# A product in the Mamba-2 chunks on VectorE instead of GpSimd, with new orders of issue at the head and in the last output projection

## The chip, the cores and the metric

One core of a Trainium2 chip runs the whole kernel. The metric is the device time of one execution in microseconds (us); of several executions the median counts. TensorE is called PE in the profile, VectorE DVE, ScalarE ACT, GpSimd POOL and SyncE SP.

## The reference

One decoder layer (DEPTH is 1) on 1024 tokens of width 1024, everything in float32. `h @ w_in` gives the columns for two branches: a convolution branch (a gated product, a causal depthwise convolution of 31 taps, a layer norm, silu, a projection) and a Mamba-2 branch (chunks of 128 tokens, 32 heads in 4 groups). Both are gated, added and projected, then a layer norm; a convolutional gated MLP and another layer norm follow.

```python
def conformer_branch(u_glu, dw_w, dw_b, ln_g, ln_b, w_out):
    a, g = jnp.split(u_glu, 2, axis=-1)
    v = a * jax.nn.sigmoid(g)
    v = causal_dwconv(v, dw_w, dw_b)
    v = jax.nn.silu(layer_norm(v, ln_g, ln_b))
    return v @ w_out

def ssd_chunked(x, dt, a_head, bm, cm):
    ...
    y_diag = jnp.einsum("bcgrls,bcsgrp->bclgrp", cb[:, :, :, None] * decay, xs)
    ...
    y_off = jnp.einsum("bclgn,bcgrpn,bcgrl->bclgrp", cc, prev, jnp.exp(a_cs))
    return (y_diag + y_off).reshape(b, t, h, p)

def reference(x, ...):
    h = layer_norm(x, ln_in_g, ln_in_b)
    for l in range(DEPTH):
        u = h @ w_in[l]
        u_glu, z, xbc, dt_raw, gate_a, gate_b = split_in(u)
        y_a = conformer_branch(u_glu, ...)
        y_b = ssd_branch(z, xbc, dt_raw, ...)
        mix = (jax.nn.sigmoid(gate_a) * y_a + jax.nn.sigmoid(gate_b) * y_b) @ w_o[l]
        h = layer_norm(DN_ALPHA * h + mix, ln1_g[l], ln1_b[l])
        ffn = conv_ffn(h, w_ffn_up[l], ffn_dw_w[l], ffn_dw_b[l], w_ffn_down[l])
        h = layer_norm(DN_ALPHA * h + ffn, ln2_g[l], ln2_b[l])
    return h
```

The line of `y_off` is the one that the change is about: C times the carried decays `exp(a_cs)`, which then meets the state that a chunk inherits.

## The kernel before

Every large matrix product is done in three passes: each float32 operand is split into a high part (fp32r, a rounded copy) and a low part (the remainder), and high x high, high x low and low x high are added up in one PSUM bank. These are lines 190, 191 and 192 (`mm3`), 128x512 each. A block of weights of 128x1024 is made by `weights` (line 151 on): SyncE loads it, ScalarE casts it (line 156), and VectorE, or whichever engine is given, subtracts (line 161).

The tokens go in two halves of 512 (`hh` 0 and 1). In each half the input projection, the 31-tap convolution (line 558, one VectorE operation per tap and 128 channels), and the mixer run together. The mixer works on 4 groups of 4 chunks each, 32 chunks in all. In a chunk of a group ScalarE makes `ab`'s exponentials for 8 heads; `m` (line 622, then line 642 on VectorE, multiplied by `cbm`, the masked product of C and B) feeds the matmuls of line 647, and `ce` (line 625 on ScalarE, then line 626, multiplied by C) those of line 650, which read the state. Every chunk but the first of the sequence has a `ce`: 28 of them. Line 632 makes `xs`, 637 `xsd`, 657 to 662 the new state, 665 and 675 the output with the skip and the gate z.

After the mixer each half has its "combine": the convolution's layer norm over channels. GpSimd adds up the channels (lines 795, 797), PE spreads the mean by a matmul (line 802), VectorE subtracts it (804), ScalarE squares (809), GpSimd adds (810), PE spreads the variance (814), and root, reciprocal, scaling, silu and the split into `sT` follow (815 to 820, 206, 207). Then the blocks `w_co` of the convolution branch's projection read `sT`. PE fills the time in between with the gate columns (`w_gb`) and the Mamba-2 branch's projection (`w_sp`).

At the head, `ln_in_first` normalises the first 512 tokens, in tiles t0 to t3 of 128, and transposes them: pair 0 is t0 and t1, pair 1 t2 and t3. Per tile: statistics (line 231, two of them), aggregation (250), root on ScalarE (251), reciprocal (254), the normalised tile `xh` (306 on VectorE or 326 on ScalarE), eight transposes on PE (328), the high part `hT_h` (341 or 347), the whole value `f` and the low part `hT_l` (353, two operations for a pair). `first_columns` multiplies the first three column blocks (line 492, 128x256): 48 matmuls with `hT_h` of pair 0, 24 with `hT_l`, then the same for pair 1. The lists kept on the way name operations: `in_order` begins with the root of t0, the root of t1, `hi` (the last `hT_h` by VectorE), `lo` and `lo_2` (the two of line 353), and the roots of t2 and t3; `parts_of[4:8]` are the statistics of t2 and t3; `los[2]` is the subtraction of the third column block, w_c_16, the only one of the three that VectorE makes; GpSimd makes the other two.

The last output projection, `out_proj_pairs`, works on the second half's tiles in two pairs (r4, r5 and r6, r7 in the text; the trace calls them all r). Each pair has four PSUM banks, 4 x 2 weight blocks `w_wo`, the residual added by line 937, and a layer norm. Around it ScalarE and VectorE split transposed rows of the first half (lines 983, 984) and copy them to `h1raw` (line 993).

What sets the order: the program is written through a tile framework that gives every operation a place in its engine's queue, by priority and by its own simulated times. Each engine then runs its queue strictly in that order and waits for semaphores. `issue_after(later, earlier)` (line 175) adds an order between two operations without a semaphore. So a changed duration or engine in one line can move operations on all engines, elsewhere too.

## Time and profile before

| | us |
|---|---|
| median of 3 runs (1938.33 to 1939.43) | 1938.6 |
| the profiled execution's own time | 1939.41 |
| its span in the trace | 1937.7 |
| VectorE busy in the stretch 500 to 560 us (half 0's combine) | 46.93 |
| VectorE busy in the stretch 750 to 1050 us (mixer of half 1) | 285.39 |
| GpSimd busy in the whole span | 215.8 |

The span runs from the first to the last instruction of the trace; the execution's own time has 1.7 us around it. The page gives the busy time of each engine, 40 slices of the span, the DMA queues, the chain of work that ended last, and groups of instructions. Other views of the same trace list what an engine waited for, single instructions in order of time (start, duration, engine, line, operation, and in brackets the idle time before it with what ended it), and the busy time of the engines in chosen stretches.

### The profile page before, as it was taken

How to read it: one execution, taken by the hardware profiler on the slowest of the kernel's cores; microseconds unless marked ns; L12 is line 12 of the kernel's file. 1: busy time of each engine (PE TensorE's matmuls, PEld its weight loads, DVE VectorE, ACT ScalarE, POOL GpSimd, SP SyncE). 2: the span in 40 equal slices, each digit the busy share in tenths (PEclk: the TensorE clock that was granted, in tenths of full speed). 3: DMA queues.
4: the chain of work that ended last, by engine and by line, in shares of the span. 5: the costliest groups of instructions: out<-in, count | busy, mean ns of one | idle time of the engine just before them, and what ended most of it. 6: DMA issues, size and time to landing. Idle time of an engine off the chain costs nothing.

```text
span 1937.7 us, 25808 instructions
## 1 busy us (share of the span) xinstructions
PE 1922.7 (99%) x9424; PEld 1571.0 (81%) x9424; DVE 1601.1 (83%) x2230; ACT 1093.0 (56%) x1642; POOL 215.8 (11%) x256
## 2 busy tenths in 40 slices
PE   9999999999999999999999999999999999999998
PEld 8888877788888788888888888878888888888886
DVE  6599999999887639899999546587788888888778
ACT  6676767663353366776765435365555555553534
POOL 1001010112300001111112140001000000022010
PEclk9999999999999999999999999999999999999999
DMA  6655555447456665556545644566455555479673
GB/s 218 218 173 201 183 197 175 166 166 265 137 180 222 211 207 184 201 180 212 177 166 163 213 151 131 181 240 231 163 164 189 179 175 187 161 275 361 201 247 115
DMA packets 127216, 376.27 MB, mean 194 GB/s; under 512 B 15184, under 2 KB 15728, under 8 KB 127088
## 3 DMA queue, kind: packets, MB, share of 16 engines
q1 hardware_dynamic: 107424, 318.48, 48.9%
q0 software_dynamic: 13184, 44.59, 6.7%
q10 hardware_dynamic: 6480, 11.55, 1.6%
q8 instruction: 74, 1.21, 0.3%
q14 instruction: 54, 0.44, 0.1%
HBM read 290.00 MB, written 84.56 MB: 193 GB/s over the span
## 4 chain that ended last, share of the span: by engine, by line
PE 82%; DVE 11%; DMA 3%; ACT 2%; issue 2%; SPq 0%; DVEq 0%; POOL 0%; ACTq 0%; POOLq 0%
PE acc L192 19%; PE acc L191 19%; PE acc L190 19%; PE sm L190 6%; PE sm L192 6%; PE sm L191 6%; DVE c L558 4%; PE sm L647 1%; DVE x L511 1%; DMA dr<-wdown 1%; PE sm L655 1%; PE sm L650 1%; DVE w_dn L1252 1%; PE acc L492 1%; DVE c L1184 1%
## 5 line engine op out<-in xcount | busy, mean ns | idle before, releaser
L192 PE MATMUL acc<-hT_h,w_c 128*128 128x512 f32 x1000 | 391.4, 392 | 0.5 <-DVE w_c L161 0.5
L190 PE MATMUL acc<-hT_h,w_c 128*128 128x512 f32 x1000 | 391.1, 391 | 0.0
L191 PE MATMUL acc<-hT_l,w_c 128*128 128x512 f32 x1000 | 391.1, 391 | 0.0
L558 DVE SCALAR_TENSOR_TENSOR c<-v,pc,c 128x512 f32<-128x512 f32 x480 | 370.6, 800 | 7.9 <-ACT c L547 5.4
L192 PEld LDWEIGHTS acc<-hT_h,w_c 128*128 128x128 f32 x1000 | 187.8, 188 | 40.9 <-issue 1.5
L190 PEld LDWEIGHTS acc<-hT_h,w_c 128*128 128x128 f32 x1000 | 187.8, 188 | 40.8 <-issue 1.9
L191 PEld LDWEIGHTS acc<-hT_l,w_c 128*128 128x128 f32 x1000 | 187.8, 188 | 39.5 <-issue 1.1
L156 ACT CAST w_c<-st_c 128x1024 fp32r<-128x1024 f32 x128 | 133.9, 1047 | 117.4 <-PE acc L192 95.4
L626 POOL TENSOR_TENSOR ce<-ce,xbc 128x1024 f32<-128x1024 f32 x28 | 77.5, 2768 | 689.6 <-ACT ce L625 689.6
L1251 ACT CAST w_dn<-dr 128x1024 fp32r<-128x1024 f32 (+1 forms) x72 | 67.4, 942 | 76.1 <-DVE dr L1184 44.2
L190 PE MATMUL sm<-h1s,w_s 128*128 128x512 f32 x264 | 102.8, 390 | 0.5 <-ACT fuv L1094 0.5
L191 PE MATMUL sm<-h1s,w_s 128*128 128x512 f32 x264 | 102.7, 389 | 0.0
L192 PE MATMUL sm<-h1s,w_s 128*128 128x512 f32 x264 | 102.2, 389 | 0.0
L615 ACT ACTIVATE m<-ab,acs 128x128 f32<-128x128 f32 x256 | 78.4, 390 | 40.8 <-PE sm L647 39.1
L161 DVE TENSOR_TENSOR w_c<-st_c,w_c 128x1024 fp32r<-128x1024 f32 x62 | 78.8, 1271 | 17.5 <-ACT w_c L156 17.4
L511 DVE SCALAR_TENSOR_TENSOR x<-u,pc,x 128x512 f32<-128x512 f32 x96 | 78.1, 828 | 5.6 <-ACT x L509 5.5
L1252 DVE TENSOR_TENSOR w_dn<-dr,w_dn 128x1024 fp32r<-128x1024 f32 (+1 forms) x72 | 77.9, 1089 | 4.7 <-ACT w_dn L1251 4.5
L192 PE MATMUL acc<-h1b_h,w_ue 128*128 128x512 f32 x176 | 68.9, 395 | 0.4 <-DVE w_ue L161 0.3
L190 PE MATMUL acc<-h1b_h,w_ue 128*128 128x512 f32 x176 | 68.8, 391 | 0.0
L191 PE MATMUL acc<-h1b_l,w_ue 128*128 128x512 f32 x176 | 68.5, 389 | 0.0
L190 PE MATMUL sm<-h1b_h,w_s 128*128 128x512 f32 x176 | 68.5, 389 | 0.0
L191 PE MATMUL sm<-h1b_l,w_s 128*128 128x512 f32 x176 | 68.5, 389 | 0.0
(369 smaller groups left out, 4554.4 us busy)
## 6 DMA issues: line engine op xcount, KB each, us to landing
st_c<-wcol SPq DMA_DIRECT2D x128, 512.0 KB, 4.4
low_scr<-w_c SPq DMA_DIRECT2D x64, 512.0 KB, 2.9
w_c<-low_scr SPq DMA_DIRECT2D x64, 512.0 KB, 4.3
ab<-acs_scr SPq DMA_DIRECT2D x32, 512.0 KB, 4.2
dr<-wdown SPq DMA_DIRECT2D x55, 256.0 KB, 4.8
st_wo<-wo SPq DMA_DIRECT2D x24, 512.0 KB, 4.1
st_ue<-wup SPq DMA_DIRECT2D x22, 512.0 KB, 3.7
first_scr<-first ACTq DMA_DIRECT2D x44, 256.0 KB, 3.0
```

Source lines behind the costliest of these rows:

```text
L156: casts.append(A.copy(w[:, 0, :], st))
L161: sub.tensor_tensor(out=w[:, 1, :], in0=st, in1=w[:, 0, :].bitcast(F32), op=ALU.subtract)
L190: TE.matmul(ps, wa(0), xa(0), start=start, stop=False, skip_group_check=more)
L191: TE.matmul(ps, wa(0), xa(1), start=False, stop=False, skip_group_check=more)
L192: TE.matmul(ps, wa(1), xa(0), start=False, stop=stop, skip_group_check=more)
L492: mm = TE.matmul(pss[o][:, ts], ws[o][:, i, k * P : (k + 1) * P], hT[:, j, k, ts], start=n == 0 and k == 0, stop=n == 2 and k == KD - 1,)
L511: V.scalar_tensor_tensor(out=o, in0=u[:, k : k + HALF], scalar=pc[:, wc + k : wc + k + 1], in1=o, op0=ALU.mult, op1=ALU.add,)
L558: V.scalar_tensor_tensor(out=accs[i], in0=v[:, k : k + HALF], scalar=pc[:, wc + k : wc + k + 1], in1=accs[i], op0=ALU.mult, op1=ALU.add,)
L615: A.activation(out=m[:, h, :], in_=ab[:, h, :], func=AF.Relu, scale=-1.0, bias=acs[:, c, 8 * g + h : 8 * g + h + 1],)
L626: G.tensor_tensor(out=ce, in0=ce, in1=CT[:, cs].unsqueeze(1).to_broadcast([P, 8, P]), op=ALU.mult)
L1251: A.copy(w[:, 0, cs], src)
L1252: V.tensor_tensor(out=w[:, 1, cs], in0=src, in1=w[:, 0, cs].bitcast(F32), op=ALU.subtract)
```

## The change

Three places are edited. First, line 626 runs on VectorE instead of GpSimd (it is line 632 after the change). Second, at the head: `xh` of t3 is made by VectorE as those of t0 and t1 are, and only t2's by ScalarE; and the orders are new: the statistics of t2 and t3 come right after `hi`, their aggregations ahead of `los[2]`, `lo` after `los[2]`; the root of t2 comes after the fourth of ScalarE's eight `f` operations (`lows`), the other four after the root of t3; and `lo_2` after `off` of t2. Third, in the last output projection the last four copies of line 993 come after the cast of the block w_wo of pair 1, kp 1, q 0. Line numbers after the change are 2 to 9 higher.

```diff
--- before.py
+++ after.py
@@ -247,7 +247,9 @@
                     part = ln_part(pl, t, st, q)
                     if keep is not None:
                         parts_of.append(part)
-            V.bn_aggr(out=mv[:, i, :], in_=st)
+            aggr = V.bn_aggr(out=mv[:, i, :], in_=st)
+            if keep is not None:
+                aggrs.append(aggr)
         root = A.activation(out=rs, in_=mv[:, :, 1], func=AF.Sqrt, bias=eps)
         if keep is not None:
             in_order.append(root)
@@ -271,7 +273,7 @@
                 q = i % 4 * P
                 TE.transpose(pt[:, q : q + P], ident, ident)
 
-    in_order, parts_of, offs = [], [], []
+    in_order, parts_of, offs, aggrs, lows = [], [], [], [], []
     in_norm = statep.tile([P, 16], F32, name="in_norm")
     in_norms = [
         (
@@ -302,7 +304,7 @@
                         t = 2 * pair + i
                         mv, rs = ln_stats(pl, xts[t : t + 1], f"in0_{t}", keep=in_norms[t])
                         xh = pl.tile([P, D], F32, tag="xh", bufs=2, name=f"xh{t}")
-                        if not pair:
+                        if t != 2:
                             V.tensor_scalar(
                                 out=xh,
                                 in0=xts[t],
@@ -343,6 +345,7 @@
                                 )
                                 if low:
                                     issue_after(by_act, last_hi)
+                                    lows.append(by_act)
                             else:
                                 by_dve = V.tensor_scalar(
                                     out=dst, in0=src, scalar1=g, scalar2=b, op0=ALU.mult, op1=ALU.add
@@ -475,14 +478,17 @@
         if hh:
             return [dt_columns(hh, hT)] + [column(hh, hT, ct) for ct in cts]
         ws = [col_weights(hh, ct, sub) for ct, sub in zip(cts, (G, G, V))]
-        _, root, hi, lo, lo_2 = in_order[:5]
+        _, root, hi, lo, lo_2, root_2, root_3 = in_order[:7]
         issue_after(casts[0], root)
-        issue_after(los[2], hi)
         for part in parts_of[4:8]:
-            issue_after(part, los[2])
-        issue_after(lo, parts_of[7])
-        for off in offs:
-            issue_after(lo_2, off)
+            issue_after(part, hi)
+        for aggr in aggrs[2:4]:
+            issue_after(los[2], aggr)
+        issue_after(lo, los[2])
+        issue_after(root_2, lows[3])
+        for low in lows[4:8]:
+            issue_after(low, root_3)
+        issue_after(lo_2, offs[0])
         pss = [bank(1) for _ in cts]
         for q in range(2):
             ts = slice(q * 256, (q + 1) * 256)
@@ -623,7 +629,7 @@
             if not first:
                 ce = pl.tile([P, 8, P], F32, tag="ce", name=f"ce{nm}")
                 A.activation(out=ce, in_=ab, func=AF.Exp)
-                G.tensor_tensor(
+                V.tensor_tensor(
                     out=ce, in0=ce, in1=CT[:, cs].unsqueeze(1).to_broadcast([P, 8, P]), op=ALU.mult
                 )
             cbm = pl.tile([P, P], F32, tag="cbm", name=f"cbm{nm}")
@@ -912,7 +918,7 @@
             mv, rstd = ln_stats(pl, rs[t : t + 1], f"o{hh}_{t}", sts[t : t + 1])
             ln_apply(rs[t], mv, rstd, 0, g, b)
 
-    def out_proj_pairs(pl, rs, mixT, g, b, done):
+    def out_proj_pairs(pl, rs, mixT, g, b, done, behind):
 
         for t in range(4):
             SY.dma_start(rs[t], h_scr[t * P : (t + 1) * P, :])
@@ -922,6 +928,8 @@
             for kp in range(4):
                 for q in range(2):
                     w = weights(wo[q, kp], f"wo1_{pair}_{q}_{kp}")
+                    while pair and kp and behind:
+                        issue_after(behind.pop(), casts[-1])
                     for t in ts:
                         for k in range(2):
                             mm3(
@@ -985,12 +993,13 @@
 
         b1 = big_tile("h1b1")
         raw = tp.tile([P, KD, HALF], F32, name="h1raw")
+        raws = []
         for t in range(4):
             ts = slice(t * P, (t + 1) * P)
             for q, pv in enumerate(by_channels(rows[t])):
                 ks = slice(4 * q, 4 * q + 4)
                 parts(lambda i: b1[:, i, ks, ts], pv)
-                A.copy(raw[:, ks, ts], pv)
+                raws.append(A.copy(raw[:, ks, ts], pv))
         sums = [qp.tile([P, 2, 4, HALF], F32R, name=f"h1s{i}") for i in (1, 2, 3)]
         rest = [tp.tile([P, D], F32, tag="row", bufs=3, name=f"r{4 + t}") for t in range(4)]
         b2, kept = [], []
@@ -1021,7 +1030,7 @@
                     parts(lambda i: b2[0][:, i, 4:8, ks], t4)
                 kept.clear()
 
-        out_proj_pairs(tp, rest, mixT, g, b, block_sums)
+        out_proj_pairs(tp, rest, mixT, g, b, block_sums, raws[-4:])
         return {
             "b11": lambda i: b1[:, i, 0:4, :],
             "b21": lambda i: b1[:, i, 4:8, :],
```

The order in which the instructions stand on the engines changes in more places than these. Three of them:

VectorE at the head. `st_in_20` and `st_in_30` are the statistics of t2 and t3, `in_norm` holds mean, variance and root of each tile, `w_c_16` is the third column block, `sm_381` to `sm_384` the banks of pair 1's transposes. Before:

```order
L347 TENSOR_SCALAR hT_h<-sm_329,gb_col 128x256
L161 TENSOR_TENSOR w_c_16_455<-st_c_16_453,w_c_16_455 128x1024
L231 BN_STATS st_in_20_385<-x_2_320 128x6 x2
L231 BN_STATS st_in_30_403<-x_3_322 128x6 x2
L250 BN_AGGR in_norm<-st_in_20_385 128x2
L353 TENSOR_TENSOR hT_l<-f_362,hT_h 128x4x256
L250 BN_AGGR in_norm<-st_in_30_403 128x2
L254 RECIPROCAL in_norm<-in_norm 128x1
L317 SCALAR_TENSOR_TENSOR off_392<-in_norm 128x1
L254 RECIPROCAL in_norm<-in_norm 128x1
L317 SCALAR_TENSOR_TENSOR off_410<-in_norm 128x1
L353 TENSOR_TENSOR hT_l<-f_362,hT_h 128x4x256
```

and after:

```order
L350 TENSOR_SCALAR hT_h<-sm_329,gb_col 128x256
L231 BN_STATS st_in_20_385<-x_2_320 128x6 x2
L231 BN_STATS st_in_30_403<-x_3_322 128x6 x2
L250 BN_AGGR in_norm<-st_in_20_385 128x2
L250 BN_AGGR in_norm<-st_in_30_403 128x2
L161 TENSOR_TENSOR w_c_16_453<-st_c_16_451,w_c_16_453 128x1024
L356 TENSOR_TENSOR hT_l<-f_362,hT_h 128x4x256
L256 RECIPROCAL in_norm<-in_norm 128x1 x2
L319 SCALAR_TENSOR_TENSOR off_392<-in_norm 128x1
L356 TENSOR_TENSOR hT_l<-f_362,hT_h 128x4x256
L308 TENSOR_SCALAR xh_409<-x_3_322,in_norm 128x1024
```

The statistics and both aggregations have moved ahead of `w_c_16`, one `off` is gone, and `xh` of t3 stands behind the second `hT_l`. On PE the 24 matmuls with `hT_l` now stand in one row, ahead of the 16 transposes of pair 1; before, eight transposes stood behind the first 12 and eight behind the second 12. On ScalarE the two roots stand between the fourth and the fifth `f`.

PE in the combine of half 0. `w_gb` are gate columns, `w_sp` blocks of the Mamba-2 branch's projection, `w_co` blocks of the convolution branch's; the matmuls of a block (24 of them) are left out behind its first. Before:

```order
L802 MATMUL sm_4703<-stats_4447,mean_w 128x512
L190 MATMUL acc_4728<-hT_h,w_gb_4_4731 128x512
...
L190 MATMUL acc_4762<-yT_2_h,w_sp_3_4765 128x512
...
L190 MATMUL acc_4794<-hT_h,w_gb_5_4797 128x512
...
L190 MATMUL acc_4828<-yT_2_h,w_sp_4_4831 128x512
...
L814 MATMUL sm_4860<-stats_4447,mean_w 128x512
L190 MATMUL acc_4897<-hT_h,w_gb_6_4900 128x512
...
L190 MATMUL acc_4931<-yT_2_h,w_sp_5_4934 128x512
...
L190 MATMUL acc_4963<-hT_h,w_gb_7_4966 128x512
...
L190 MATMUL acc_4997<-yT_2_h,w_sp_6_5000 128x512
...
L190 MATMUL acc_5031<-yT_2_h,w_sp_7_5034 128x512
...
L190 MATMUL acc_5067<-sT_4864,w_co_0_5070 128x512
```

and after:

```order
L808 MATMUL sm_4701<-stats_4445,mean_w 128x512
...
L190 MATMUL acc_4826<-yT_2_h,w_sp_4_4829 128x512
...
L190 MATMUL acc_4895<-hT_h,w_gb_6_4898 128x512
...
L190 MATMUL acc_4929<-yT_2_h,w_sp_5_4932 128x512
...
L190 MATMUL acc_4961<-hT_h,w_gb_7_4964 128x512
L820 MATMUL sm_4858<-stats_4445,mean_w 128x512
L191 MATMUL acc_4961<-hT_l,w_gb_7_4964 128x512
...
L190 MATMUL acc_4995<-yT_2_h,w_sp_6_4998 128x512
...
L190 MATMUL acc_5029<-yT_2_h,w_sp_7_5032 128x512
...
L190 MATMUL acc_5065<-sT_4862,w_co_0_5068 128x512
...
L190 MATMUL acc_5101<-sT_4862,w_co_1_5104 128x512
...
L190 MATMUL acc_5065<-sT_4862,w_co_0_5068 128x512
```

The matmuls of the mean (802, now 808) and of the variance (814, now 820) stand later against the blocks: between the variance's and the first with `sT` stood 120 matmuls, and now 71. The first 12 of `w_co_0` are now followed by some of `w_co_1` and `w_co_2`, where before `w_co_0` ran to its end. Half 1's combine has the same distances as before.

PE at the start of pair 1 of the last output projection. `acc_10862` and `acc_10864` (after: 10860, 10862) are the banks of r6 and r7 for q 0, `acc_10863` (10861) that of r6 for q 1; the two numbers in `w_wo` behind the pair's 1 are q and kp. Before:

```order
L190 MATMUL acc_10862<-w_wo_1_0_0_10868,mixT_h 128x512
...
L190 MATMUL acc_10862<-w_wo_1_0_1_10902,mixT_h 128x512
L190 MATMUL acc_10864<-w_wo_1_0_0_10868,mixT_h 128x512
...
L190 MATMUL acc_10864<-w_wo_1_0_1_10902,mixT_h 128x512
L190 MATMUL acc_10863<-w_wo_1_1_0_10885,mixT_h 128x512
...
L191 MATMUL acc_10862<-w_wo_1_0_1_10902,mixT_h 128x512
...
L191 MATMUL acc_10864<-w_wo_1_0_1_10902,mixT_h 128x512
...
L190 MATMUL acc_10863<-w_wo_1_1_1_10919,mixT_h 128x512
```

and after:

```order
L190 MATMUL acc_10860<-w_wo_1_0_0_10866,mixT_h 128x512
...
L190 MATMUL acc_10860<-w_wo_1_0_1_10900,mixT_h 128x512
L190 MATMUL acc_10862<-w_wo_1_0_0_10866,mixT_h 128x512
...
L190 MATMUL acc_10862<-w_wo_1_0_1_10900,mixT_h 128x512
L191 MATMUL acc_10860<-w_wo_1_0_1_10900,mixT_h 128x512
...
L191 MATMUL acc_10862<-w_wo_1_0_1_10900,mixT_h 128x512
...
L190 MATMUL acc_10861<-w_wo_1_1_0_10883,mixT_h 128x512
...
L190 MATMUL acc_10861<-w_wo_1_1_1_10917,mixT_h 128x512
```

The ten matmuls that end the block `w_wo_1_0_1` have moved ahead of those of the third bank. On VectorE the subtraction of that block now stands ahead of both halves of r5 (line 937), where it stood between them, and on ScalarE its cast stands right behind the last cast of line 983, with the four copies of line 993 behind it (before: two ahead of it, two behind).

In a chunk of the mixer the new product stands on VectorE a few operations ahead of the product for `m`: in group 2's chunk 3 of half 1, for instance, two operations of the convolution lie between the two.

## The prediction

> **What bounds the kernel.** I read the page first, then the list of TensorE's own waits, because the engine shares say that only those can be shortened.
>
> ```profile
> span 1937.7 us, 25808 instructions
> PE 1922.7 (99%) x9424; PEld 1571.0 (81%) x9424; DVE 1601.1 (83%) x2230; ACT 1093.0 (56%) x1642; POOL 215.8 (11%) x256
> PEclk9999999999999999999999999999999999999999
> PE acc L492 <- DVE hT_l L353: 1.4, 1, 1.4
> ...
> PE acc L190 <- ACT w_wo L156: 0.7, 1, 0.7
> PE acc L190 <- DVE r L937: 0.7, 1, 0.7
> PE sm L647 <- DVE m L642: 0.6, 1, 0.6
> ...
> PE acc L192 <- DVE w_c L161: 0.5, 1, 0.5
> ```
>
> TensorE is busy for 99% of the span at a granted clock that never leaves the top digit. The change leaves every matmul in the program, so it can only take away waits, or add some. The rows are waits of PE (us in all, times, longest). Each happened once. Those in a stage that the change touches are L492 (1.4, the head), L190 behind w_wo and behind r (0.7 each, the last output projection), L647 behind m (0.6, a mixer) and L192 behind w_c (0.5, a mixer): 1.4 + 0.7 + 0.7 + 0.6 + 0.5 = 3.9 us. That is 0.2% of the span, which is about what a measurement of this kernel can tell from no change. So "faster by more than 0.2%" needs nearly every one of them to vanish and nothing to come in its place.
>
> **Part 1: the product of the decays on VectorE.** VectorE looks like the wrong place for more work: in the mixers it is all but full.
>
> ```profile
> 100.00:500.00 400.00, 399.50 (x2118) 321.46 (x2116) 395.13 (x581) 258.48 (x437) 47.34 (x32) 1.00 0.54 186
> L626 POOL TENSOR_TENSOR ce<-ce,xbc 128x1024 f32<-128x1024 f32 x28 | 77.5, 2768 | 689.6 <-ACT ce L625 689.6
> L642 DVE TENSOR_TENSOR m<-m,cbm 128x1024 f32<-128x1024 f32 x32 | 38.7, 1210 | 0.4 <-ACT m L622 0.4
> L558 DVE SCALAR_TENSOR_TENSOR c<-v,pc,c 128x512 f32<-128x512 f32 x480 | 370.6, 800 | 7.9 <-ACT c L547 5.4
> L511 DVE SCALAR_TENSOR_TENSOR x<-u,pc,x 128x512 f32<-128x512 f32 x96 | 78.1, 828 | 5.6 <-ACT x L509 5.5
> L558 DVE SCALAR_TENSOR_TENSOR c<-v,pc,c x480: 658/750/2908, 92.4 to 1081.8; 128x512 f32<-128x512 f32 x160
> 980.11 2.99 POOL L626 TENSOR_TENSOR ce<-ce,xbc 128x1024 f32<-128x1024 f32 x1 [16.45 <-ACT ce L625]
> 980.76 3.55 DVE L558 SCALAR_TENSOR_TENSOR c<-v,pc,c 128x512 f32<-128x512 f32 x2
> 984.23 1.21 DVE L642 TENSOR_TENSOR m<-m,cbm 128x1024 f32<-128x1024 f32 x1
> ```
>
> In the stretch 100 to 500 us (columns PE, PEld, DVE, ACT, POOL) VectorE is busy for 395.13 of 400 us. The 28 products take 2768 ns each on GpSimd. On VectorE the nearest row is L642, with the same shape, type and broadcast operand: 1210 ns. Added: 28 x 1.21 = 33.9 us of VectorE time.
>
> But busy is not working. An L558 takes 750 ns at the median (the row with min/median/max) and up to 2908. The row at 980.76 shows why: two of them began while GpSimd's product ran (980.11 to 983.10) and took 3.55 us where two at the median take 1.50. The first evidently stood until the product was through: a stall of 2.05 us. How much there is in all I estimate from the means: L558's lies 50 ns above the median, 480 x 0.050 = 24.0 us, and L511's, an operation of the same kind and shape, 78 ns, 96 x 0.078 = 7.5. Together 31.5 us, 1.1 per product, with rarer lines on top. So VectorE gives 33.9 and gets back about as much. Bounds for its net: +33.9 (none of the excess is GpSimd's) and 33.9 - 77.5 = -43.6 us (it stands for all of GpSimd's time). I take zero, since 31.5 is nearest to the rows. The product itself is ready 2.77 - 1.21 = 1.6 us sooner after its exponential.
>
> [...]
>
> On TensorE's path this touches two waits. The one for m (0.6 in the list above) was for the product of 984.23. Without GpSimd that would start 2.05 us sooner, and with the new product queued ahead of it 1.21 later: 0.84 sooner, which covers the wait. Gain 0.6. The 0.5 behind w_c has no such margin, and I leave it. All other chunks already had m in time. Since the new product stands in VectorE's queue, it makes what follows wait if its exponential is late; that was never so for m by more than 0.4 us in all (L642's idle). I take -0.6, bounds -1.1 to +1.
>
> **Part 2: the head.** The rows are those of the head (start, us, engine, line).
>
> ```profile
> 8.51 0.81 DVE L306 TENSOR_SCALAR xh<-x,in_norm 128x1024 f32<-128x1024 f32 x1
> 9.08 4.85 POOL L161 TENSOR_TENSOR w_c<-st_c,w_c 128x1024 fp32r<-128x1024 f32 x2 [6.64 <-ACT w_c L156]
> 10.32 1.90 DVE L347 TENSOR_SCALAR hT_h<-sm,gb_col 128x256 fp32r<-128x256 f32 x4 [1.00 <-PE sm L328]
> 11.30 6.00 PE L492 MATMUL acc<-hT_h,w_c 128*128 128x256 f32 x48
> 12.14 2.87 DVE L161 TENSOR_TENSOR w_c<-st_c,w_c 128x1024 fp32r<-128x1024 f32 x1
> 12.72 3.75 ACT L341 ACTIVATE f<-sm,gb_col 128x256 f32<-128x256 f32 x8
> 14.93 2.46 DVE L231 BATCH_NORM_STATS2 st_in<-x 128x6 f32<-128x512 f32 x4
> 17.42 1.17 DVE L353 TENSOR_TENSOR hT_l<-f,hT_h 128x1024 fp32r<-128x1024 f32 x1
> 18.64 1.70 PE L492 MATMUL acc<-hT_l,w_c 128*128 128x256 f32 x12 [1.35 <-DVE hT_l L353]
> 18.96 2.38 ACT L326 ACTIVATE xh<-x,off,in_norm 128x1024 f32<-128x1024 f32 x2
> 20.26 1.09 PE L328 MATMUL sm<-ident,xh 128*128 128x128 f32 x8
> 21.11 1.67 PE L492 MATMUL acc<-hT_l,w_c 128*128 128x256 f32 x12
> 22.61 1.04 PE L328 MATMUL sm<-ident,xh 128*128 128x128 f32 x8
> 23.63 0.62 PE L492 MATMUL acc<-hT_h,w_c 128*128 128x256 f32 x3
> ```
>
> Before, L161 stands from 12.14 to 15.01 on GpSimd's two (9.08 to 13.93), then come the statistics (to 17.39) and L353 (to 18.59): PE runs out at 17.30 and starts at 18.64. Now the four statistics stand first: 12.22 + 2.46 = 14.68, two aggregations to about 15.0. L161 then finds GpSimd done (13.93) and takes L642's 1.21, to 16.2. L353 ends at 16.2 + 1.17 = 17.4. PE's third weight block needs L161's result for the last 8 of the 48 matmuls, at 11.30 + 40 x 6.00/48 = 16.3, so just in time. PE starts hT_l at 17.4. It then runs both groups of 12 in a row (1.62 and 1.50 us by the starts above), which needs the second L353 by 19.0: it follows the first within about 0.3 us, to 18.9. Then xh of t2 (ScalarE, 1.19 each, behind f at 16.5 and two roots: about 17.7 to 18.9) and of t3 (VectorE, the 0.81 of L306: to 19.7) are there before the transposes at 20.5. These take 0.85, then 1.02 to the first hT_h: 22.4 where it was 23.63. Gain 1.2 us.
>
> What hides the rest is thin: 0.1 us at 16.3 and at 19.0. If the statistics, too, stood until 13.93, L161 would end at 17.9, L353 at 19.1, and PE would start 0.4 later than before. BN_STATS reads one tensor, L558 and L161 two, so I take 1.2, bounds -1.5 to +0.4.
>
> **Part 3: the last output projection.**
>
> ```profile
> 1270.48 1.05 ACT L156 CAST w_wo<-st_wo 128x1024 fp32r<-128x1024 f32 x1
> 1271.08 0.68 DVE L937 SCALAR_TENSOR_TENSOR r<-r,acc 128x512 f32<-128x512 f32 x1
> 1273.59 0.69 DVE L937 SCALAR_TENSOR_TENSOR r<-r,acc 128x512 f32<-128x512 f32 x1 [1.24 <-DMA r<-h_scr]
> 1274.33 0.50 PE L190 MATMUL acc<-w_wo,mixT_h 128*128 128x512 f32 x1 [0.65 <-DVE r L937]
> ```
>
> The cast that PE waited for (to 1271.53) moves ahead of the last four L993 copies, two of which ran just before it, so it comes about 1.1 us sooner. But the next output bank is only freed by the L937 of 1271.08, which ends at 1271.76: little of that 0.7 goes, 0.1. The second wait is for the DMA of r5. In the new order PE has 10 more matmuls of the other bank before it needs that bank: 10 x 0.23 = 2.3 us of cover for 0.65. Gain 0.1 + 0.65, say 0.8; bounds 0 to -1.4. Four copies later cost nothing while ScalarE is 56% busy; if their banks were wanted at once, one copy is 0.6 us.
>
> **Part 4: what moves unasked.** In half 0's combine PE's matmul of the variance (L814) stands later, and only 71 matmuls are left between it and the first that reads sT, where there were 120.
>
> ```profile
> L814 PE MATMUL sm<-stats,mean_w x4: 592/592/592, 535.8 to 1162.0; 128*128 128x512 f32 x4
> 549.36 0.69 DVE L207 TENSOR_TENSOR sT<-cc,sT 128x512 fp32r<-128x512 f32 x1 [0.85 <-ACT sT L206]
> 559.54 0.68 DVE L207 TENSOR_TENSOR sT<-c,sT 128x512 fp32r<-128x512 f32 x1
> 563.87 0.39 PE L190 MATMUL acc<-sT,w_co 128*128 128x512 f32 x1
> 565.00 0.39 PE L192 MATMUL acc<-sT,w_co 128*128 128x512 f32 x1
> ```
>
> The last two rows are five matmuls apart: 1.13/5 = 0.226 us each. From L814 at 535.8 the first slice of sT took 14.25 us (to 550.05), the eighth 24.4 (to 560.22); PE came at 28.1. Now PE comes at about 71 x 0.226 + 0.6 = 16.6 us: the first slice is 2.4 early, the eighth is late unless PE has other matmuls. In the old order of w_co the eighth is wanted after 7 x 3 matmuls, at 16.6 + 4.8 = 21.4, so 3 us late in sum (24.4 - 21.4). In the new order matmuls of w_co_1 and w_co_2 stand between, up to some 30 of them, which covers most of the 3. I take +0.5, bounds 0 to +3.5.
>
> **Sum.** -0.6 - 1.2 - 0.8 + 0.5 = -2.1 us against the profiled execution's own 1939.41 us, which is 0.8 above the median of the runs shown, 1938.6. On the median: 1936.5.
>
> **The rivals.** First, everything goes and nothing comes: all 3.9 us of the listed waits, and what PE loses in starting again (in the head the 12 matmuls after a wait took 1.62 us to the next start, the other 12 took 1.50: 0.1 each, five times): -4.4, 1934.2. For it: VectorE's stalls end everywhere, so the order planned for it is kept. Against it: the bank at 1271.76 and the w_c wait have no margin.
> Second, sT comes late: PE waits in half 0 for the whole 3 to 3.5 us, the head gives only half: -0.6 - 0.6 - 0.8 + 3.3 = +1.3: 1939.9. It decides at the sixth to eighth slice of sT; for it speaks the cover that shrank from 28.1 to 16.6 us, against it the interleaving. [...]
> Third, slower: VectorE becomes the bound in the mixers. If the stalls given back are only 0.6 us per product, VectorE falls behind by 28 x 0.6 = 17 us over the mixers, and m (behind the new product in the same queue) reaches PE late. The one late m cost 0.6; if half of the 28 chunks did so, 14 x 0.6 = 8.4, less the 2.0 of head and projection: +6.4, 1945.0. It decides where the product ends after PE's L647 is due. Against it: one wait for m in 32 chunks, though stalls fell into most of them.
> Fourth, the head gives nothing (the statistics do stand behind GpSimd): -0.6 + 0.4 - 0.8 + 0.5 = -0.5: 1938.1.
>
> **Numbers.** Forecast 0.50; first rival 0.14; second 0.13; third 0.08; fourth 0.15. The likeliest is 1936.5. Bounds summed on the good side (-1.1 - 1.5 - 1.4) are -4.0, 1934.6; the range goes down to 1934.0 for the first rival, and up to 1941.0 over the second and fourth, leaving out the third and the far end of the second. Faster by over 0.2% (under 1934.7) in most of the first rival: 0.10. Slower by over 0.2% (above 1942.5) in the third: 0.08. Within: 0.82.
>
> **What would show it.** L558 with no case above 1 us in the mixers while VectorE's busy share there stays near 99%; PE's wait for hT_l gone and L492 resuming near 22.4; no wait for r in the projection, one of 0.6 for a bank; a new wait of PE for sT under 1 us near 560. I am wrong if PE waits for m or ce in many chunks, or for sT by more than 2 us.

## The result and the profile after

The changed kernel takes 1942.48 us (median of 22 runs, 1938.48 to 1945.35), the kernel before 1938.43 (22 runs beside them, 1936.21 to 1939.90). The ratio is 1.0019, with a 95% interval of 1.0013 to 1.0025: a loss of 4 us where a gain of 2.1 was forecast, and 1.5 us above the top of the range. The profiled execution took 1944.78 us, 2.3 above the median of its kernel, so the trace below shows a bad case of the loss.

First the page's head and the list of PE's own waits (us in all, times, longest).

```profile
span 1942.8 us, 25771 instructions
PE 1926.2 (99%) x9424; PEld 1571.9 (81%) x9424; DVE 1596.3 (82%) x2258; ACT 1086.5 (56%) x1637; POOL 139.4 (7%) x228
```

```profile
PE sm L808 <- POOL stats L803: 2.2, 1, 2.2
PE acc L191 <- DVE w_dn L1261: 2.2, 1, 2.2
PE sm L274 <- POOL ident masks.py:199: 1.7, 1, 1.7
PE acc L192 <- DVE w_gb L161: 1.3, 1, 1.3
PE acc L192 <- DVE w_co L161: 0.5, 1, 0.5
PE sm L190 <- ACT fuv L1103: 0.5, 1, 0.5
```

All five waits that the prediction added up (hT_l, w_wo, r, m, w_c) are gone. Three new ones stand in the combine of half 0: for the sum over channels that the mean is made of (L808 behind GpSimd's L803), for the gate block w_gb, and a short one for a weight block w_co. The one for w_dn, in the MLP, was 0.9 before.

The head did what was forecast (start, us, engine, line):

```profile
11.34 6.12 PE L498 MATMUL acc<-hT_h,w_c 128*128 128x256 f32 x46
17.30 3.04 PE L498 MATMUL acc<-hT_l,w_c 128*128 128x256 f32 x24
...
22.07 6.25 PE L498 MATMUL acc<-hT_h,w_c 128*128 128x256 f32 x48
```

PE goes into hT_l at 17.30 with no wait, runs the 24 in a row, and is back at hT_h at 22.07, where it was 23.63 before and 22.4 was forecast: 1.6 us gained.

The loss is here, in half 0's combine, on PE and GpSimd:

```profile
527.43 0.39 PE L190 MATMUL acc<-hT_h,w_gb 128*128 128x512 f32 x1
530.02 1.12 PE L808 MATMUL sm<-stats,mean_w 128*128 128x512 f32 x2 [2.21 <-POOL stats L803]
...
531.77 0.63 PE L190 MATMUL acc<-hT_h,w_gb 128*128 128x512 f32 x1
532.20 0.63 PE L191 MATMUL acc<-hT_l,w_gb 128*128 128x512 f32 x1
...
528.70 1.27 POOL L803 TENSOR_TENSOR stats<-stats,c 128x512 f32<-128x512 f32 x1 [9.30 <-DVE c L564]
```

The numbers in brackets are the idle time before the row and what ended it. PE stands for 2.21 us because GpSimd adds the last channels of the convolution only at 528.70. Then PE runs on, but its matmuls start 0.43 us apart (531.77, 532.20), where 0.226 is what the prediction's rows gave. The windows view (PE, PEld, DVE, ACT, POOL, granted clock) says why:

```profile
531.00:532.00 1.00, 1.00 (x4) 0.82 (x3) 1.00 (x2) 0.00 (x0) 0.00 (x0) 0.52 0.40 139
532.00:533.00 1.00, 1.00 (x3) 0.78 (x3) 1.00 (x3) 0.64 (x1) 0.00 (x0) 0.50 0.44 80
533.00:534.00 1.00, 1.00 (x4) 0.76 (x3) 1.00 (x3) 0.66 (x1) 0.00 (x0) 0.50 0.75 270
534.00:535.00 1.00, 1.00 (x5) 0.83 (x4) 1.00 (x3) 1.00 (x3) 0.00 (x0) 0.77 0.45 180
```

The granted clock is half for more than 3 us: 0.48 + 0.50 + 0.50 + 0.23 = 1.7 us of work lost behind a wait of 2.2. The wait for w_dn was followed by half clock as well (0.57 on average from 1790 to 1794 us, another 1.7):

```profile
1788.07 0.69 DVE L1193 TENSOR_TENSOR dr<-dr,c 128x512 f32<-128x512 f32 x1 [2.79 <-DMA dr<-wdown]
1789.95 0.50 PE L191 MATMUL acc<-w_dn 128*128 128x512 f32 x1 [2.20 <-DVE w_dn L1261]
```

VectorE waited there for a weight that a DMA brought late. In the traces of the other kernels below this wait is between none and 1.6 us, with the product on either engine, so I don't count it as the change's. What it has over the kernel before (1.3 us) and its half clock (1.7) are 3.0 us of the +5.1 in this trace. Without them it would stand at +2.1, so the median run, at +4, loses something that this trace doesn't show. The account of the trace, by my own sums: listed waits 5.6 us before and 6.7 after (ident apart, which is 1.7 in both), +1.1; half clock twice, +3.4; together +4.5 of the span's +5.1.

Why does the convolution end late? The last taps of half 0, GpSimd's last sum and the matmuls of the mean (first and last start, both halves) before, and the last taps after:

```profile
505.36 2.32 DVE L558 SCALAR_TENSOR_TENSOR c<-v,pc,c 128x512 f32<-128x512 f32 x3
...
507.83 1.30 POOL L797 TENSOR_TENSOR stats<-stats,c 128x512 f32<-128x512 f32 x1 [10.09 <-DVE c L558]
```

```profile
L802 PE MATMUL sm<-stats,mean_w x4: 592/592/592, 513.2 to 1139.3; 128*128 128x512 f32 x4
```

```profile
527.02 1.53 DVE L564 SCALAR_TENSOR_TENSOR c<-v,pc,c 128x512 f32<-128x512 f32 x2
```

From 507.7 to 528.6: 20.9 us later. GpSimd's sum ended at 509.1 before and PE's matmul stood at 513.2, so 4 us were all the room there was. The new order put that matmul behind 67 more matmuls, 15 us, which is about 2 short. That the product costs VectorE time isn't the reason, since it gives as much back (first fence: ns of one as min/median/max, first and last start; second: busy us and mean ns):

```profile
L564 DVE SCALAR_TENSOR_TENSOR c<-v,pc,c x480: 649/745/1782, 90.9 to 1090.5; 128x512 f32<-128x512 f32 x160
L632 DVE TENSOR_TENSOR ce<-ce,xbc x28: 1209/1218/1231, 79.6 to 1070.7; 128x1024 f32<-128x1024 f32 x28
```

```profile
L564 DVE SCALAR_TENSOR_TENSOR c<-v,pc,c 128x512 f32<-128x512 f32 x480 | 350.1, 755 | 14.4 <-ACT c L553 12.1
L517 DVE SCALAR_TENSOR_TENSOR x<-u,pc,x 128x512 f32<-128x512 f32 x96 | 70.2, 746 | 5.2 <-ACT x L515 5.1
```

A product takes 1218 ns on VectorE. The taps fell by 370.6 - 350.1 = 20.5 us and L511 (now L517) by 78.1 - 70.2 = 7.9, 28.4 together where 31.5 was estimated; VectorE's busy time over the whole span even fell, from 1601.1 to 1596.3 us. What grew is the time in which it stands idle: in the stretch from 300 us to the old end of the convolution it was busy for 205.40 us before (first fence) and is for 193.95 after (second).

```profile
300.00:508.00 208.00, 207.50 (x1078) 167.20 (x1077) 205.40 (x293) 118.26 (x187) 29.39 (x23) 1.00 0.53 183
```

```profile
300.00:508.00 208.00, 206.68 (x1074) 166.48 (x1073) 193.95 (x282) 112.38 (x181) 14.57 (x16) 1.00 0.52 177
```

From 90 us to the last tap of half 0 the windows view of single lines gives: product +13.4, taps -9.0, L511 -4.0, squares -1.8, operations that now come ahead of the last taps (four more weight blocks, four additions of the combine) +7.5, idle time +14.9 (7.0 to 21.8). The two largest parts of the idle time have names in the list of VectorE's waits up to that point, before (first fence) and after (second):

```profile
DVE w_c L161 <- ACT w_c L156: 2.5, 1, 2.5
DVE c L558 <- ACT c L547: 1.8, 2, 1.0
```

```profile
DVE c L564 <- ACT c L553: 10.1, 4, 5.8
DVE w_c L161 <- ACT w_c L156: 5.2, 8, 1.8
```

The longest wait for c, 5.78 us, in the rows of VectorE, ScalarE and the queue of SyncE:

```profile
466.85 2.08 DVE L564 SCALAR_TENSOR_TENSOR c<-v,pc,c 128x512 f32<-128x512 f32 x3 [5.78 <-ACT c L553]
...
466.00 0.82 ACT L553 ACTIVATE c<-v,pc 128x512 f32<-128x512 f32 x1 [6.43 <-DMA c_scr<-c]
...
460.01 0.70 SPq L574 DMA_DIRECT2D c_scr<-c  x1
```

The convolution keeps its accumulators `c` in two buffers. When two channel tiles are done they are stored (L574), and the next two may begin (L553 on ScalarE) only when the store has left the buffer, 6 us later here. My reading is that VectorE was often behind before and had other taps in hand, while now it arrives early and waits, so that the time that GpSimd's stalls gave back was lost again to ScalarE and a DMA. The rows show the waits; that they make the convolution late is tested below.

The w_gb wait, a little earlier, has two sides. VectorE's rows after (first fence) and before (second):

```profile
481.82 6.88 DVE L564 SCALAR_TENSOR_TENSOR c<-v,pc,c 128x512 f32<-128x512 f32 x4
488.62 2.31 DVE L161 TENSOR_TENSOR w_gb<-st_gb,w_gb 128x1024 fp32r<-128x1024 f32 x1
```

```profile
482.50 6.51 DVE L558 SCALAR_TENSOR_TENSOR c<-v,pc,c 128x512 f32<-128x512 f32 x5
488.93 1.22 DVE L161 TENSOR_TENSOR w_gb<-st_gb,w_gb 128x1024 fp32r<-128x1024 f32 x1
```

Four taps took 6.88 us where four at the median take 2.98, while GpSimd was making its sums over channels (L801 and L803) beside them, and the subtraction for a block that PE wanted was queued behind them. But taps were slowed there before, too (five took 6.51), and the subtraction ended at 490.15 then and at 490.93 now, only 0.8 us later. PE, for its part, reached the block at 489.1 instead of 491.4, since it no longer loses the waits ahead of this point. The wait of 1.3 us is made of both.

### The profile page after: what moved, and what is told of

It reads as the page before. It is cut to its first block, busy times and chain, and to the rows that moved or that the text cites. A ratio compares the mean times of both kernels' runs of the same rounds, so it can differ in the third digit from the quotient of the medians.

```text
span 1942.8 us, 25771 instructions
## 1 busy us (share of the span) xinstructions
PE 1926.2 (99%) x9424; PEld 1571.9 (81%) x9424; DVE 1596.3 (82%) x2258; ACT 1086.5 (56%) x1637; POOL 139.4 (7%) x228
## 3 DMA queue, kind: packets, MB, share of 16 engines
q10 hardware_dynamic: 6480, 11.55, 1.6%
q8 instruction: 74, 1.21, 0.3%
## 4 chain that ended last, share of the span: by engine, by line
PE 88%; DVE 6%; DMA 3%; issue 1%; ACT 1%; POOL 0%; SPq 0%; DVEq 0%; ACTq 0%; POOLq 0%
PE acc L192 21%; PE acc L191 21%; PE acc L190 20%; PE sm L190 6%; PE sm L191 6%; PE sm L192 6%; DVE c L564 2%; DMA dr<-wdown 2%; PE sm L653 2%; PE sm L661 1%; PE sm L656 1%; PE acc L498 1%; PE sm L614 1%; DMA c_scr<-c 1%; DVE w_dn L1261 0%
## 5 line engine op out<-in xcount | busy, mean ns | idle before, releaser
L564 DVE SCALAR_TENSOR_TENSOR c<-v,pc,c 128x512 f32<-128x512 f32 x480 | 350.1, 755 | 14.4 <-ACT c L553 12.1
L517 DVE SCALAR_TENSOR_TENSOR x<-u,pc,x 128x512 f32<-128x512 f32 x96 | 70.2, 746 | 5.2 <-ACT x L515 5.1
L703 POOL DMA_DIRECT2D nrm_scr<-rows x8 | 4.8, 594 | 917.7 <-DVE rows L701 917.7
```

Source lines behind the costliest of these rows:

```text
L517: V.scalar_tensor_tensor(out=o, in0=u[:, k : k + HALF], scalar=pc[:, wc + k : wc + k + 1], in1=o, op0=ALU.mult, op1=ALU.add,)
L564: V.scalar_tensor_tensor(out=accs[i], in0=v[:, k : k + HALF], scalar=pc[:, wc + k : wc + k + 1], in1=accs[i], op0=ALU.mult, op1=ALU.add,)
```

## The experiments

The theory with which they began: the product in half 0 makes the convolution end late, PE waits for it in the combine, and the wait takes the clock down. What spoke against it, and what came in its place as runs fell otherwise, stands in the expectations as it was held at the time.

### Which part, which half

The three parts of the change alone, and head and projection together:

```diff
ce_only:    G.tensor_tensor(out=ce, ...)  ->  V.tensor_tensor(out=ce, ...)
head_only:  the orders and xh of the head, nothing else
proj_only:  the copies of L993 behind the cast, nothing else
head_proj:  head_only and proj_only
```

> Only the product of the carried decays moves to VectorE; head and last output projection as before. Theory A (the loss is made in half 0's combine: VectorE's filler, the convolution, ends some 20 us later, PE stands about 2 us before the matmul of the mean and then runs some 3.4 us at half clock, and a w_gb block is late by 1.3): slower than before by about 4.05 + 1.5 + 1.3 = 6 to 7 us, about 1945, with a wait of PE for the statistics of 1.5 to 3 us and a granted clock near 0.5 behind it. Theory B (the loss is made at the end, where PE waits for a w_dn block, and comes from the new times of the transfers after the head and projection edits): 0 to -1 us, the wait for the mean small.

> Only the edits at the head. Theory A: -1.3 to -1.6 us (PE starts the second half of the head's matmuls at 22.1 instead of 23.6, as in the changed kernel's trace) and nothing else. Theory B: the gain of the head is there, but the wait for w_dn near 1785 us grows by about 1 us or more, so -0.5 to +2 us.

> Only the edit of the last output projection. Theory A: -1.0 to -1.5 us, no wait of PE for w_wo or r near 1271 us. Theory B: -0.5 to +2 us, with a longer wait for w_dn near 1785 us.

> The changed kernel with the product left on GpSimd: head and projection edits alone. Theory A: the sum of the two, -2.3 to -3.0 us (about 1935.8), no wait for the mean, clock 1.00 around 530 us. Theory B: 0 to +3 us, with the wait for w_dn at 2 us and half clock behind it, as in the changed kernel.

Against 1939.45 us of the kernel before (30 runs): the product alone 1944.78, ratio 1.0033 (1.0022 to 1.0043); the head alone 1938.40, 0.9991 (0.9982 to 1.0000); the projection alone 1938.69, 0.9997 (0.9988 to 1.0006); both together 1936.98, 0.9987 (0.9978 to 0.9996). So two parts of the three bring 2.5 us together, where 2.0 were forecast, and the product by itself costs 5.3. Of the two the projection alone can't be told from no change, and the head alone only just. In the product's trace the wait has changed places: 2.8 us for w_gb and 0.7 for the mean, 3.5 in sum as in the changed kernel (1.3 and 2.2), again with one half clock, here behind w_gb. I take it for one delay, which PE meets at the first of two places; the runs of this part don't show that.

Then the product by halves of the sequence, with head and projection as before or as changed:

```diff
ce_h0:     (G if hh else V).tensor_tensor(out=ce, ...)
ce_h1:     (V if hh else G).tensor_tensor(out=ce, ...)
hp_ce_h1:  ce_h1 together with head_proj
```

> The product on VectorE in half 0 only (12 of the 28); head and projection as before. Theory A1 (the loss is in half 0's combine, because VectorE's filler has no slack there: the mean's statistics and the next w_gb block come late): the same +5 us as with all 28, between +4 and +6.5. Theory A2 (the loss comes from the product anywhere, by its 1.2 us of VectorE time in every chunk): 12/28 of it, about +2.3.

> The product on VectorE in half 1 only (16 of the 28). Theory A1: no loss, the wait of 0.6 for m in half 1 goes: -0.8 to 0 us. Theory A2: 16/28 of the loss, about +3.

> Head and projection edits, and the product on VectorE in half 1 only. Theory A1: the -2.5 us of head and projection and some -0.6 on top, about -3 (1936.4 against 1939.4), the best of all. Theory A2: -2.5 + 3 = +0.5.

Against 1939.90 us (21 runs): in half 0 alone 1944.56, 1.0029 (1.0019 to 1.0040); in half 1 alone 1939.36, 0.9991 (0.9983 to 1.0000). By the time all of the loss is half 0's. The trace of ce_h0 doesn't show it: it is of the fastest of its 10 executions (1940.93 us), with 0.7 us of waiting for the mean, none for w_gb and no half clock, so what the slower ones lose there was not seen. Half 1 has the same product and the same queue, and in the changed kernel its convolution, too, ends 9 us later, but there it doesn't matter; the first and last start of taps and of the mean's matmuls show the room:

```profile
L564 DVE SCALAR_TENSOR_TENSOR c<-v,pc,c x240: 650/745/754, 735.3 to 1090.5; 128x512 f32<-128x512 f32 x120
...
L808 PE MATMUL sm<-stats,mean_w x4: 592/592/697, 530.0 to 1143.5; 128*128 128x512 f32 x4
```

In half 1 the taps end 52 us ahead of the mean. The version that keeps GpSimd in half 0 and takes the rest of the change, hp_ce_h1, is the fastest of all that ran: 1935.38 us (6 runs), 0.9975 (0.9964 to 0.9987), faster than both kernels. Its list of PE's waits has neither the mean nor w_gb:

```profile
PE acc L191 <- DVE w_dn L1261: 0.9, 1, 0.9
PE acc L190 <- DVE r L945: 0.8, 1, 0.8
```

### Does a wait of about 2 us halve the clock?

A kernel by itself: 84 bursts of 45 to 61 matmuls 128x512; between two bursts PE waits for one to seven ScalarE operations, in the second half with a short one behind.

```diff
+for half in (0, 1):
+    for k in range(1, 8):
+        for rep in range(6):
+            ps = bank(1)
+            for j in range(burst):
+                TE.matmul(ps, w[:, :P], xr, start=j == 0, stop=j == burst - 1)
+            for i in range(k):
+                A.activation(out=w, in_=ps, func=AF.Identity, scale=0.001)
```

> Not the layer, but a kernel of 84 bursts of 45 to 61 matmuls 128x512, with a wait for 1 to 7 ScalarE operations between two (six times each, and again with a shorter operation added); the output holds a copy of x. [...]

A burst of 52 matmuls behind a wait of 1.95 us, and one behind 2.26:

```profile
192.55 13.69 PE L138 MATMUL acc<-xr,w 128*128 128x512 f32 x52 [1.95 <-ACT w L142]
...
862.89 12.08 PE L138 MATMUL acc<-xr,w 128*128 128x512 f32 x52 [2.26 <-ACT w L144]
```

They took 13.69 us once and 12.08 once: the burst behind the shorter wait was slowed (granted clock 0.73 from 195 to 197 us), the other not. Counted over all bursts (own sums from the starts), by the idle time that the trace gives:

| wait of PE, us | bursts slowed |
|---|---|
| up to 1.63 | 0 of 24 |
| 1.95 | 4 of 6 |
| 2.26 | 3 of 6 |
| 2.58 | 2 of 6 |
| 2.88 | 5 of 6 |
| 3.21 | 4 of 6 |
| 3.5 and more | 29 of 29 |

A slowed burst lost 1.4 to 1.8 us in most cases, and up to 3.0 behind the longer waits; an unslowed one 0.1. So a wait of 2.2 us costs either 2.2 or about 3.9, and which it is varies between bursts of one execution. What decides it was not shown. That fits the spread of the changed kernel. A half clock of 1.7 us takes 0.0009 off the mean clock of a run; its nine runs with a mean clock of 0.999 have a median of 1940.5 us, the eleven with 0.998 one of 1942.9, and the two with 0.997 took 1944.8 and 1945.35. So by this estimate some 2 us of the loss stand without any half clock, and each half clock adds about 2. Waits of the kernels themselves agree: 2.75 us for w_gb in ce_only was followed by half clock (0.81 on average from 492 to 495 us, 0.62 from 495 to 498), 2.60 for w_gb in mean_late (below) was not (1.00 from 489 to 500).

### What makes the convolution late

If the two buffers of `c` are the cause, a third one should take VectorE's waits away. To make room, `yb` goes from two buffers to one. The same edit stands on the changed kernel, on the kernel before as a control, and on ce_only.

```diff
-            c = statep.tile([P, HALF], F32, tag="c", bufs=2, ...)
+            c = statep.tile([P, HALF], F32, tag="c", bufs=3, ...)
-                ya = pl.tile([P, HALF], F32, tag="yb", bufs=2, ...)
+                ya = pl.tile([P, HALF], F32, tag="yb", bufs=1, ...)
```

> The changed kernel with three buffers instead of two for the convolution's accumulators c (and one instead of two for yb in the combine, to make room). It takes away what VectorE's first taps wait for, the store of the channel before last. Theory R1 (the convolution ends late because VectorE stands idle for that buffer: 10.1 us of waits for c's first tap before 529 us): those waits fall under 3 us, the convolution of half 0 ends 8 us earlier or more, no wait of PE for the mean above 0.5 us, and the time is that of the head and projection edits plus the mixer's gain: -2.5 to -4 us against before. Theory R2 (VectorE simply has too much work there, or waits for other things): the wait for the mean or for w_gb stays at 2 us or more and the time stays +2 to +5 us.

> The kernel before with the same three and one buffers. R1 and R2 alike: VectorE waited only 1.8 us for c's first tap before, and PE did not wait for the mean, so nothing to gain there: -0.5 to +0.5 us.

> Only the product on VectorE (head and projection as before), with three buffers for c and one for yb. R1 (waiting for c's buffer makes the convolution late): waits for c's first tap under 3 us, no wait for the mean over 0.5 us; if the new order brings no other wait, -1 to +1 us against before (the product alone had +5.3). R2: the wait for the mean or for a w_gb block stays, +4 us or more.

The control is unmoved: 1938.06 (beside 1939.21), 0.9996 (0.9987 to 1.0005). c3_after took 1943.87 (7 runs, beside 1939.21), 1.0029 (1.0018 to 1.0040); c3_ce_only 1945.44 (5 runs, beside 1939.31), 1.0036 (1.0022 to 1.0049). By the time this failed in both; the traces say more. VectorE's wait for c in c3_after (first fence), and its waits for c and for the weight blocks in c3_ce_only (second):

```profile
DVE c L564 <- ACT c L553: 1.0, 1, 1.0
```

```profile
DVE w_c L161 <- ACT w_c L156: 11.8, 12, 2.2
DVE c L558 <- ACT c L547: 3.5, 2, 2.5
```

In c3_after VectorE's waits for `c` fell from 10.1 to 1.0 us, the convolution ended at 522.1 instead of 528.6 (6.5 us earlier, for the 8 of theory R1), and PE waits neither for the mean nor for w_gb. That fits the buffers as part of the cause. c3_ce_only doesn't: its waits for `c` fell from the 11.3 us of ce_only to 3.5, but those for the weight blocks rose from 5.4 to 11.8, VectorE's idle time from 90 us to the last tap stayed (23.7 us for 23.8), and the convolution ended at 529.3 for 531.4. PE waits neither for the mean nor for w_gb there either. So what makes the convolution late is not shown: when VectorE no longer waits for one thing, it waits for the next.

With other buffers the framework also plans all queues anew, and in both kernels a new wait of 4.4 us came at another place (here c3_after):

```profile
323.60 0.80 PE L190 MATMUL acc<-hT_h,w_c 128*128 128x512 f32 x1 [4.39 <-ACT x L515]
...
319.67 1.28 ACT L631 ACT_TABLE_LOAD   x1
320.96 1.06 ACT L631 ACTIVATE ce<-ab 128x1024 f32<-128x1024 f32 x1
321.93 1.04 ACT L628 ACTIVATE m<-m 128x1024 f32<-128x1024 f32 x1
322.87 1.82 ACT L515 ACTIVATE x<-acc,pc 128x512 f32<-128x512 f32 x3
```

PE needs a bank that ScalarE's L515 empties, and in ScalarE's queue a table load and two exponentials now stand ahead of it. The clock is at half behind it, too (0.50 from 324 to 328 us, 3.4 us of work lost between 323 and 330). The time of these two runs therefore says nothing on the buffers.

### Moving only what waits

So I left buffers and engines as the change has them, and moved single operations. mean_late puts the mean's matmul of half 0 later on PE, into the block w_sp 4; order_fixed does that and also moves two taps behind the subtraction of the block w_gb that PE had waited for.

```diff
 mean_late, on the changed kernel:
+                if j == 4 and not hh:
+                    issue_after(mean_mm[0], steps[2])
 order_fixed, on top of it:
+                if not hh and (i, k) in ((6, 14), (7, 5)):
+                    taps.append(tap)
 ...
+                while j == 2 and taps:
+                    issue_after(taps.pop(), los[-1])
```

> The changed kernel with one more order of issue: in half 0 PE's matmul of the mean stands behind the third group of three matmuls of the block w_sp 4, 14 matmuls (3.2 us) later than before; everything ahead of it on PE is as in the changed kernel. Theory A3 (the loss at this place is the wait of 2.2 us and the half clock behind it, 1.7 us where it strikes): the wait for the mean falls under 0.5 us, the clock stays at 1.00 there, and the time is 2 to 4 us under the changed kernel's +4.05, so between 0 and +2 us against before. Theory A4 (the delay of the convolution must be paid somewhere: sT is late instead): a new wait for sT of 2 us or more and the time stays at +3 to +5.

> The kernel with the mean placed later, and one more order of issue: in half 0 two of the convolution's taps (the four that stood on VectorE between the blocks w_sp 0 and w_gb 2 follow) come behind the subtraction of w_gb 2 instead of ahead of it. PE's order is the same. Theory A5 (with its late convolution VectorE reaches the subtraction of w_gb 2 too late, and that and the mean are all that half 0 loses): PE's wait for w_gb, 2.6 us in that kernel's trace, falls under 0.5 us, no new wait over 1 us comes for the mean or for sT, and the time is 1.5 to 3.5 us under that kernel's, -1 to -3.5 us against before. Theory A6 (VectorE's lag only moves to the next thing that waits for it): another wait of 1.5 us or more before 600 us, and the time stays within 1 us of before.

mean_late took 1939.46 us beside 1939.31 of the kernel before, 1.0004 (0.9995 to 1.0012). In its trace the wait for the mean is gone and none for `sT` has come, though the combine runs still later; the clock stays whole there (1.00 from 520 to 550 us); what is left is the w_gb block:

```profile
PE acc L192 <- DVE w_gb L161: 2.6, 1, 2.6
```

So from +4.05 to +0.15 against the kernel before, by the place of a single matmul: the wait for the mean with its half clock is worth 3 to 4 us (2.9 by the ratios, 3.9 by the differences). The queues around it moved a little as well, as the 2.6 us for w_gb in place of 1.3 show. order_fixed: 1938.78 beside 1939.13, 0.9999 (0.9990 to 1.0008). Its profiled execution was the fastest of its 11 runs, 1935.5 us, and the largest waits in PE's list there, after ident's, are:

```profile
PE sm L190 <- ACT fuv L1112: 0.5, 1, 0.5
PE acc L190 <- DVE r L954: 0.5, 1, 0.5
```

The trace shows both waits gone, as theory A5 has it, but the median has only 0.35 us of the 1 to 3.5 that were expected, which is where theory A6 put it. Against head_proj (0.9987) some 2.3 us stay open. It is hardly half clock, since only one of the 11 runs has a mean clock below 0.999; where the others lose it no trace shows. VectorE still waits 9.6 us for `c` in this trace, on stores that take between 2.0 and 8.6 us in the changed kernel, so a late store could bring the waits back in some executions; that is an argument and was not shown.

## Why the prediction was wrong

**Bounds and list.** Right: only waits could be gained, and all five that were named did go. The second price of a new wait, the half clock behind it (1.7 us in the changed kernel's trace), stood in no term of the sum.

**Part 1, the product.** Its price was right (1.218 us for 1.21), and so was the guess of what GpSimd's stalls would return (28.4 us for 31.5). The longest tap fell from 2908 to 1782 ns when the product left GpSimd. The wait for m went, as forecast, and the one for w_c too. **The step that failed is the inference from a net of zero on VectorE to nothing behind it being late: the term of -0.6, with +1 as its worst, gave no price to the path from the last tap over GpSimd's sum to the matmul of the mean.** On that path the runs showed the last tap 20.9 us later and a wait of 2.2 us with a half clock of 1.7 behind it. A sum of busy time doesn't say when a queue is done. The taps fill VectorE's gaps and end last; time that a faster tap gives back is only worth something if the next operation is ready. In half 0 some 15 us came back, and 15 more stood idle. Which of VectorE's waits decides that stays open, as the tests with three buffers showed.

**Part 4, what moves unasked.** The same error shows again. The prediction priced the last link of the combine, `sT`, at +0.5 with bounds to +3.5, and didn't ask what feeds it. `sT` was late in no trace. What was late is the first link, the mean, which needs the last tap; it had 4 us of room before, in rows that the prediction did not look at. In place of -0.6 + 0.5 the product cost 5.3 alone, and by the difference to head_proj (1.0019 against 0.9987) about 6.2. In the traces some 3.5 of that are the two waits and 1.7 a half clock. Neither sign that the prediction had named for being wrong, m or ce late in many chunks or sT late by over 2 us, came.

**Parts 2 and 3.** The head: -1.6 in the trace for -1.2 forecast. That the statistics would not stand behind GpSimd's subtractions was an estimate: in the trace before they did not run beside those. After the change they did (GpSimd from 8.95 to 13.78 us, the four statistics from 11.55) and took 2.54 us, for 2.46 before. The projection: both waits of the list are gone, 1.4 us for the 0.8 forecast, but that the one for r went is in part luck: with the same edit it was 1.1 us in head_proj and 0.8 in hp_ce_h1. Together -2.5 by the time, for -2.0. The fourth rival (the head gives nothing) is out.

**The rivals.** The third, slower by VectorE, had the sign, and +6.4 where +4.05 came, but by m in the mixers, and PE never waited for m. The second had the stage, half 0's combine, but the wrong tile. The rival that was missing: if the time given back can't be used, the product's 13.4 us push back the last taps of half 0, and the mean has 4 of room.

## What to carry to other kernels

When work moves onto a nearly full engine in a strict queue, price the end of its filler and not its busy sum: find what reads the filler last, and how much room it has in each stage; half 1 had over 50 us and half 0 had 4. Time that ended stalls give back is a gain only where the queue has other work ready; up to the last tap of half 0 VectorE's idle time grew here by 14.9 us. In a program whose queues are planned by a simulation, a single move changes all of them, so split a change by stage before judging it: all of this one but the product of half 0 was worth keeping.

## What the runs showed that I had not expected

PE's clock fell to half behind waits of 2.2 us in the changed kernel (0.50 from 532 to 534 us). In the stand-alone kernel bursts were slowed behind waits of 1.95 to 3.21 us sometimes (18 of 30), from 3.5 us on always (29 of 29), up to 1.63 never (0 of 24). Where the half clock begins differs as well: by the granted clock of the windows it was 1.0 and 0.6 us after PE had resumed in the changed kernel (0.52 from 531 to 532 us, 0.78 from 1790 to 1791), as it resumed in ce_only, and 0.6 us before the end of the wait of 4.4 in c3_after (0.74 from 322 to 324).

Sums on GpSimd of 128x512 stood beside four taps that took 6.88 us instead of 2.98. Five took 6.51 in the kernel before, at the same place. So in these traces taps were slow beside GpSimd's sums, as two of them were beside its product before (3.55 us at 980.76), and VectorE's queue has not lost all of these stalls.
